# Queries and keys of the attention's second group as Strassen products behind the values, kept in DRAM

## The chip, the cores and the metric

The kernel runs on one core of a Trainium2 chip. A core has five engines: TensorE (PE: matrix products, with its weight loads listed apart as PEld), VectorE (DVE), ScalarE (ACT), GpSimd (POOL) and SyncE (SP), which here issues every DMA. Each engine works through its own instructions in program order, and engines wait for each other by semaphores. The metric is the device time of one execution in microseconds; the kernel before has a median of 1728.54 us over three runs (1725.78 to 1728.69).

## What is computed

A trunk of two layers over a sequence of 1024 rows of width 1024 in float32. The first layer is attention with three dilation groups (windows of 128, 512 and 2048 at dilations 1, 4 and 16), 16 heads of 64; the second is a state-space layer. The change touches the first.

```python
def dilated_attention_mixer(h, w_in, w_out, rel_bias):
    proj = h @ w_in                       # 1024 x (9 * 1024 + 1024)
    qkv = proj[..., :9 * 1024].reshape(B, S, 3, 3, 16, 64)   # q/k/v, group, head
    z = proj[..., 9 * 1024:]
    for g, (window, dilation) in enumerate(((128, 1), (512, 4), (2048, 16))):
        o, l = dilated_group_attention(qkv[:, :, 0, g], qkv[:, :, 1, g],
                                       qkv[:, :, 2, g], rel_bias, window, dilation)
        outs.append(o); lses.append(l)
    wts = softmax(stack(lses), axis=0)
    o = sum(wts[..., None] * stack(outs), axis=0)
    return (o * silu(z)) @ w_out
```

`dilated_group_attention` takes each residue of the position modulo the dilation by itself, in blocks of 128 queries against the same and the previous block of keys, with a bias, a mask, the softmax and its log-sum.

## The kernel before

**Precision.** A float32 factor is split into two parts, hi and lo, in a rounded 32-bit type (`split`: ACT casts the hi part, L83; DVE or POOL subtracts it for the lo part, L84). A product of two split factors takes three matmuls (hi·hi, hi·lo, lo·hi). `h` is held split in SBUF as `hh` and `hl`.

**The V phase** (`v_phase`, roughly the first 345 us) normalises and transposes the rows and computes the values of all groups and the gates. From the second chunk on the values are Strassen products (`Quads.values`): the operands are cut in quarters, `quad` makes seven products of quarters instead of eight, with sums of weight quarters on DVE ahead of each and sums of results behind it. It goes to DRAM (`v_dr`). Preparations for the second layer (`prep.powers`, `prep.products`) are hung on the running count of products, on products 8 + 3·et and 10 + 3·et.

**The attention** (roughly 345 to 1155 us) loops over eight pairs of heads, `attn_pair`. In a pair, for each of three groups g:

- The query weights are loaded (`load_w`, `wraw`, 512 KB on SP), split (`whi` on ACT, `wlo` on POOL), and multiplied: two halves of 24 matmuls 128x512 (`proj_half`, L110), each into a `psj` bank, of which there are two. `evac_q` (L200/201) scales, reorders by residue and splits the result into `qh`/`ql`. The same for the keys (`evac_k`: kh L83, kl L84, L214).
- `load_bias` loads a bias tile `T`, `load_v` the values `vp`, which are split to `vs`.
- Two units u = 0, 1 of four query tiles each (`attn_unit`): scores (L485, bank `psl`), bias and maximum on DVE (L488), exponentials on ACT (L499; each also shows as a read of its accumulator), transposes on PE (L510, `pt`), split into `ph` (hi on ACT, lo on DVE), the product with the values (L559 or L585, `pso`), copied to `O` by ACT (L569) and added there by DVE (L570).
- `put_ms` transposes maxima and sums (`ptm`, L597) and stores them (L604 in the last group).

**The merge** of a pair runs inside the next one: `merge_weights` loads maxima and sums (`cm`, L620), makes weights and stores them (L633); when the next pair comes to its second group, `merge` loads them three times (`mw`, L648, two DMAs each), multiplies the three `O` on POOL (L697) and adds them (L699). There are four `O` buffers, so the next pair's second `O` cannot be written before POOL has freed one.

**Order.** The scheduler fixes each engine's order when the program is built. It places weight splits and evacuations early, as they carry a high priority (`AHEAD`). All DMAs are issued on SP's one queue, in program order.

Of the kernel before, what the change touches and what calls it, by code (L numbers as in the profile page):

```python
# [15 lines left out]
F32 = mybir.dt.float32  # L16
# [7 lines left out]
P = 128  # L24
# [3 lines left out]
H = 512  # L28
NEG = -1.0e30
EPS = 1e-6  # L30

AHEAD = 600

# [146 lines left out]
def load_bias(c, p, g):  # L180


    t = c.attn.tile([P, 2, 256], F32, tag="T", name="T", bufs=2)
    at = 0 if g < 2 else P
    src = bass.AP(c.vec_dr.tensor, c.vec_dr.offset + (g * 16 + 2 * p) * 384 + at, [[1, P], [384, 2], [1, 256 - at]])
    c.nc.sync.dma_start(t[:, :, at:256], src)
    return t
# [26 lines left out]
            c.nc.scalar.copy(dh[HEADS[1 - s]], sv[HEADS[s]])  # L214


def zero_other(c, t):

    for s in range(2):
        rows = HEADS[1 - s]  # L220
        c.nc.gpsimd.tensor_copy(t[rows, s, :], c.zt[rows].to_broadcast([64, S]))


def load_first(c, a, k):
# [35 lines left out]
class Quads:  # L260
# [4 lines left out]
    def __init__(self, c):  # L265
        nc = c.nc
        self.c = c

        def part(th, kh):
            return [t[:, 4 * kh:4 * kh + 4, :] for t in c.h[th]]  # L270

        add, sub = ALU.add, ALU.subtract

        def tt(o, x, y, op):
            nc.vector.tensor_tensor(o, x, y, op=op)

# [24 lines left out]
        t2, t3 = c.vslot(2, F32), c.vslot(3, F32)  # L301
        self.sums = [t2[:, 0:2], t2[:, 2:4], t3[:, 0:2]]
        self.tmp = t3[:, 2:4].rearrange("p a x -> p (a x)")


    done, jobs = 0, {}

    def quad(self, raw, order, product, banks, use):
# [3 lines left out]
        c, nc = self.c, self.c.nc  # L312
        b11, b12, b21, b22 = raw
        n = b11.shape[2]
        tmp = self.tmp[:, 0:4 * n].rearrange("p (k x) -> p k x", k=4)

        def sub(o, x, y):
            nc.vector.tensor_tensor(o, x, y, op=ALU.subtract)
# [79 lines left out]
        self.quad(quarters, [0, 1, 5, 6, 4, 3, 2], product, banks, use)  # L398


def gates(c, a, h, es):
# [36 lines left out]

def load_v(c, p, g):
# [18 lines left out]
def ms_col(g, n, h, qt):  # L458

    return (n * 16 + h * 8 + 7 - qt, n * 16 + h * 8 + (qt ^ 1), n * 16 + h * 8 + qt)[g]  # L460


def attn_unit(c, g, u, q, k, v, bt, ms, O):
# [7 lines left out]
    for j in range(4):  # L471
        qt = u * 4 + j
        m = (7 - qt, 1 - qt % 2, 0)[g]
        start = (max(m - 1, 0) * P, qt // 2 * 256, qt * P)[g]
        w = 256 if m else 128
        tiles.append(w)
        ps = c.psl.tile([P, 2, 256], F32, tag="psl", name="psl")
# [6 lines left out]
        for n, (o, a, b) in enumerate(jobs):  # L484
            nc.tensor.matmul(o, a[:, qs], b, start=n == 0, stop=n == len(jobs) - 1, skip_group_check=True)  # L485
        for h in range(2):
            col = ms_col(g, 0, h, qt)
# [148 lines left out]
def big(c, p, name):  # L636

    if p == 7:
        return c.wraw.tile([P, S], F32, tag="wraw", name=name)
    return c.attn.tile([P, S], F32, tag="mw", name=name, bufs=2)  # L640


def weights_of(c, p, g):
# [5 lines left out]
    return w  # L649


def attn_pair(c, p, w_in, h):
    nc = c.nc
    c.pair = p
    O = []
    for g in range(3):
        qh = c.attn.tile([P, S], F32R, tag="qh", name="qh", bufs=2)
        ql = c.attn.tile([P, S], F32R, tag="ql", name="ql", bufs=2)
        w = load_w(c, w_in[g * 8 + p])
        for th in range(2):  # L660
            src = proj_half(c, w, h[th])
            with c.tc.high_priority(AHEAD):
                evac_q(c, src, g, th * H, (qh, ql))
        bt = load_bias(c, p, g)
        if g == 2:
            zero_other(c, c.kh)
        w = load_w(c, w_in[(3 + g) * 8 + p])
        for th in range(2):
            src = proj_half(c, w, h[th])
            with c.tc.high_priority(AHEAD):  # L670
                evac_k(c, src, g, th * H, c.kh, c.kl)
# [38 lines left out]
def attention(c, a):  # L710
# [36 lines left out]
    zt = c.cst.tile([P, 1], F32, name="zt")  # L747
    nc.vector.memset(zt, 0.0)
    c.zt = zt
    zero_other(c, c.kl)  # L750
    c.w_engine = nc.gpsimd
    for p in range(8):
        attn_pair(c, p, a["w_in"], h)
# [702 lines left out]
def trunk(tc, a):  # L1456
# [4 lines left out]
    with ExitStack() as es:  # L1461
# [12 lines left out]
        dram = lambda name, shape: c.dr.tile(shape, F32, name=name)  # L1474
        c.vec_dr = dram("vec_dr", [3, 16, 384])
        c.v_dr = dram("v_dr", [3, 2, S, H])
        c.ms_dr = dram("ms_dr", [8, 3, 4, S])
        c.wt_dr = dram("wt_dr", [8, 3, 2, S])
        c.on_dr = dram("on_dr", [8, P, S])
# [137 lines left out]
```

## Time and profile before

| what | value |
|---|---|
| median of three runs | 1728.54 us |
| the profiled execution's own time | 1722.86 us |
| its span in the trace | 1721.1 us |
| PE busy | 1655.9 us (96%) |
| DVE busy | 1064.8 us (62%) |
| ACT busy | 799.9 us (46%) |
| POOL busy | 483.5 us (28%) |
| moved by DMA | 212.68 MB |
| one head pair, from one store of L604 to the next | 96.6 us |

In a line of the timeline stand the start in us, the time, the engine, the line of the kernel, what is written from what, the shapes and how many were taken together, and in brackets the idle time ahead and who ended it. A matmul's own duration overlaps the next one's; what one costs is the distance from start to start.

### The profile page before, as it was taken

How to read it: one execution, taken by the hardware profiler on the slowest of the kernel's cores; microseconds unless marked ns; L12 is line 12 of the kernel's file. 1: busy time of each engine (PE TensorE's matmuls, PEld its weight loads, DVE VectorE, ACT ScalarE, POOL GpSimd, SP SyncE). 2: the span in 40 equal slices, each digit the busy share in tenths (PEclk: the TensorE clock that was granted, in tenths of full speed). 3: DMA queues.
4: the chain of work that ended last, by engine and by line, in shares of the span. 5: the costliest groups of instructions: out<-in, count | busy, mean ns of one | idle time of the engine just before them, and what ended most of it. 6: DMA issues, size and time to landing. Idle time of an engine off the chain costs nothing. (4 is left out here: it accounts for less than half of the span.)

```text
span 1721.1 us, 25792 instructions
## 1 busy us (share of the span) xinstructions
PE 1655.9 (96%) x9262; PEld 1415.1 (82%) x9262; DVE 1064.8 (62%) x2582; ACT 799.9 (46%) x1872; POOL 483.5 (28%) x321
## 2 busy tenths in 40 slices
PE   6999999999999999999999999988998999989998
PEld 5889999988888788888888888876886887867886
DVE  7698798735566556566555565557462777764533
ACT  5232222246656656656756756653442232243411
POOL 2000000041242432524342442405210344413121
PEclk9999999999999999999999999999999999999999
DMA  6223454441242323323232423327259766465432
GB/s 236 91 52 102 137 181 154 128 144 53 55 111 80 87 80 91 88 74 105 79 107 73 116 81 98 112 71 200 86 166 232 206 211 219 139 186 167 141 122 86
DMA packets 176900, 212.68 MB, mean 124 GB/s; under 512 B 37361, under 2 KB 133380, under 8 KB 176772
## 3 DMA queue, kind: packets, MB, share of 16 engines
q1 hardware_dynamic: 176772, 211.04, 40.9%
q8 instruction: 73, 1.20, 0.3%
q14 instruction: 55, 0.45, 0.1%
HBM read 154.03 MB, written 56.96 MB: 123 GB/s over the span
## 5 line engine op out<-in xcount | busy, mean ns | idle before, releaser
L110 PE MATMUL psj<-hh,whi 128*128 128x512 f32 x896 | 360.4, 402 | 16.2 <-ACT kh L214 8.5
L110 PE MATMUL psj<-hh,wlo 128*128 128x512 f32 x896 | 359.6, 402 | 0.3 <-POOL wlo L84 0.3
L110 PE MATMUL psj<-hl,whi 128*128 128x512 f32 x896 | 357.9, 399 | 0.0
L110 PEld LDWEIGHTS psj<-hh,whi 128*128 128x128 f32 x896 | 169.8, 189 | 51.6 <-ACT kh L214 10.6
L84 POOL TENSOR_TENSOR wlo<-wraw,whi 128x1024 fp32r<-128x1024 f32 x48 | 115.4, 2405 | 335.7 <-ACT whi L83 329.4
L110 PEld LDWEIGHTS psj<-hh,wlo 128*128 128x128 f32 x896 | 169.6, 189 | 35.8 <-POOL wlo L84 0.7
L110 PEld LDWEIGHTS psj<-hl,whi 128*128 128x128 f32 x896 | 169.8, 190 | 33.5
L499 ACT ACTIVATE lg<-lg,nm 128x128 f32<-128x128 f32 (+1 forms) x384 | 168.1, 440 | 18.9 <-DVE nm L494 18.0
L83 ACT CAST whi<-wraw 128x1024 fp32r<-128x1024 f32 x80 | 83.8, 1047 | 141.9 <-PE psj L110 97.4
L488 DVE CUSTOM_DVE_ANT_0 lg<-psl,T 128x128 f32<-128x128 f32 (+1 forms) x384 | 115.8, 346 | 53.5 <-PE psl L485 52.1
L84 DVE TENSOR_TENSOR ph<-pt,ph 128x512 fp32r<-128x512 f32 (+2 forms) x160 | 97.2, 621 | 37.4 <-ACT ph L83 35.3
L389 PE MATMUL psq<-whi,v 128*128 128x256 f32 x640 | 118.7, 283 | 0.0
L110 PE MATMUL psj<-h1h,whi 128*128 128x512 f32 (+1 forms) x272 | 107.0, 394 | 10.3 <-DVE z L1402 7.9
L84 DVE TENSOR_TENSOR kl<-psj,kh 64x512 fp32r<-64x512 f32 x96 | 66.0, 688 | 70.7 <-ACT kh L83 70.0
L570 DVE TENSOR_TENSOR O<-O,pso 64x512 f32<-64x512 f32 x64 | 44.2, 691 | 103.3 <-ACT O L569 102.6
L110 PE MATMUL psj<-h1l,whi 128*128 128x512 f32 (+1 forms) x272 | 105.4, 388 | 0.2 <-DVE h1l L84 0.2
L110 PE MATMUL psj<-h1h,wlo 128*128 128x512 f32 (+1 forms) x272 | 105.0, 387 | 0.0
L389 PEld LDWEIGHTS psq<-whi,v 128*128 128x128 f32 x640 | 99.5, 189 | 1.0 <-ACT whi L83 0.6
L83 ACT CAST ph<-pt 128x512 fp32r<-128x512 f32 (+2 forms) x160 | 81.6, 533 | 35.9 <-PE pt L510 34.7
L510 PE MATMUL pt<-identr,lg 128*128 128x128 f32 x560 | 93.5, 275 | 0.0
L559 PE MATMUL pso<-ph,vs 128*128 128x256 f32 (+1 forms) x544 | 89.9, 275 | 2.8 <-ACT ph L83 1.5
L559 PEld LDWEIGHTS pso<-ph,vs 128*128 128x128 f32 x544 | 81.6, 189 | 13.1 <-ACT ph L83 2.6
(287 smaller groups left out, 3862.7 us busy)
## 6 DMA issues: line engine op xcount, KB each, us to landing
wraw<-in_w_in_dram SPq DMA_DIRECT2D x56, 512.0 KB
mw<-wt_dr SPq DMA_DIRECT2D x48, 256.0 KB
v<-in_w_v_dram SPq DMA_DIRECT2D x20, 512.0 KB
vp<-v_dr SPq DMA_DIRECT2D x16, 512.0 KB
wraw<-in_ssm_w_in_dram SPq DMA_DIRECT2D x16, 512.0 KB
v_dr<-v SPq DMA_DIRECT2D x30, 256.0 KB
rot_dr<-rt SPq DMA_DIRECT2D x48, 128.0 KB
ca_dr<-ca SPq DMA_DIRECT2D x32, 144.0 KB
```

The lines of the kernel that those rows point to most:

```text
L83: nc.scalar.copy(hi, src)
L84: return (engine or nc.vector).tensor_tensor(lo, src, f32(hi), op=ALU.subtract)
L110: nc.tensor.matmul(ps, a[:, s], b[:, k, :], start=first and k == 0 and n == 0, stop=k == KT - 1 and n == 2, skip_group_check=True)
L389: nc.tensor.matmul(o, r[x][:, k, ts], w[y][:, k, :], skip_group_check=True, start=i in (0, 4, 5) and t % 2 == k == n == 0, stop=k == 3 and ...
L488: nc.vector.tensor_tensor_reduce(lg[:, h, j, 0:w], ps[:, h, 0:w], bt[:, h, 256 - w:256], scale=1.0, scalar=-3.0e38, op0=ALU.add, op1=ALU.m ...
L499: nc.scalar.activation(lg[:, h, j, 0:w], lg[:, h, j, 0:w], AF.Exp, bias=nm[:, h, b:b + 1], accum_out=ms[:, col:col + 1])
L510: c.nc.tensor.transpose(pt[:, n * P:(n + 1) * P], lg[:, h, j, part * P:part * P + P], c.ident)
L559: nc.tensor.matmul(o, l, r, start=n == 0, stop=n == len(jobs) - 1, skip_group_check=True)
L570: nc.vector.tensor_tensor(dst, dst, fr[1], op=ALU.add)
```

## The change

The queries and keys of the second group (g = 1, `MADE`) are no longer computed in `attn_pair`. They are computed right behind the values, in the V phase, by a new `Quads.tiles`: for each pair it loads its query and its key weights (two tiles of 512 KB), and makes seven Strassen products of quarters, each of 12 matmuls 128x512, where the attention had four halves of 24. Results are scaled, put in order by residue and split (`put_q`, `put_k`, `halves`), and stored hi and lo in DRAM (`q_dr`, `kk_dr`; ten DMAs and 2 MB a pair). The attention loads them per unit, eight DMAs and 1.25 MB each, into `mq`, `mkh` and `mkl`, of which there is one buffer each (`load_made`). Three other buffers change: `ph` has two instead of three, `mw` one instead of two, and `T` takes a slot of the ring with the tag "a", which has three. The preparations are hung on products 8 + 5·et and 11 + 5·et.

```diff
+MADE = 1
@@ load_bias
-    t = c.attn.tile([P, 2, 256], F32, tag="T", name="T", bufs=2)
+    t = c.slot("T", tag="a").rearrange("p (h x) -> p h x", h=2)
+def halves(c, p, src, scale=None):
+    if p < 6:
+        t = c.wraw.tile([P, 2, H], F32R, tag="wraw", name="qks")
+        hi, lo = t[:, 0], t[:, 1]
+    else:
+        hi, lo = (c.slot(x, F32R, tag="b") for x in ("qkh", "qkl"))
+    hi, lo = (x.rearrange("p (r l) -> p r l", r=src.shape[1]) for x in (hi, lo))
+    split(c, hi, lo, src, scale)
+    return hi, lo
+def put_q(c, p, th, t):
...
+    hi, lo = halves(c, p, t.rearrange("p (l r) -> p r l", r=o)[:, :, ::-1], 0.125)
...
+    for x in range(2):
+        nc.sync.dma_start(bass.AP(dr.tensor, off + x * 192 * S, [[S, 64]] + cols), f32(hi[HEADS[x]]))
+    nc.sync.dma_start(bass.AP(dr.tensor, off + 64 * S, [[S, P]] + cols), f32(lo))
+def put_k(c, p, th, t):
...
+    for x, v in enumerate(halves(c, p, t.rearrange("p (l r) -> p r l", r=o))):
+        off = c.kk_dr.offset + (p * 2 + x) * P * S + th * n
+        c.nc.sync.dma_start(bass.AP(c.kk_dr.tensor, off, [[S, P], [S // o, o], [1, n]]), f32(v))
+def load_made(c, p, u):
+    q, kh, kl = c.made
+    cols = slice(u * H, u * H + H)
+    for x in range(2):
+        nc.sync.dma_start(f32(q[:, x]), c.q_dr[p, x, :, cols])
+    for x in range(2):
+        for rows in HEADS:
+            nc.sync.dma_start(f32(kh[rows, x]), c.kk_dr[p, 0, HEADS[x], cols])
+        nc.sync.dma_start(f32(kl[HEADS[x], x]), c.kk_dr[p, 1, HEADS[x], cols])
+    return (q[:, 0], q[:, 1]), (kh, kl)
@@ class Quads
+    def tiles(self, srcs, use):
+        self.turn ^= 1
+        raw = c.vslot(10 + self.turn, F32).rearrange("p (n a) x -> p n (a x)", n=2)
+        for n, s in enumerate(srcs):
+            nc.sync.dma_start(raw[:, n], s)
...
+        def product(i, r, w, acc):
+            for k in range(4):
+                for n, (x, y) in enumerate(((0, 0), (0, 1), (1, 0))):
+                    nc.tensor.matmul(acc[0], w[x][:, k, :], r[y][:, k, :], skip_group_check=True,
+                                     start=i in (0, 4, 5) and k == n == 0, stop=k == 3 and n == 2)
...
+        self.quad(quarters, [0, 5, 1, 6, 4, 3, 2], product, banks, lambda th, nh, b, t: use(th, nh, t))
@@ v_phase
-        q.jobs.setdefault(8 + 3 * et, []).append(lambda et=et: prep.powers(et))
-        q.jobs.setdefault(10 + 3 * et, []).append(lambda et=et: prep.products(et))
+        q.jobs.setdefault(8 + 5 * et, []).append(lambda et=et: prep.powers(et))
+        q.jobs.setdefault(11 + 5 * et, []).append(lambda et=et: prep.products(et))
     for ch in range(2, 6):
         q.values(a, ch)
+    for p in range(8):
+        q.tiles([a["w_in"][(3 * x + MADE) * 8 + p] for x in range(2)],
+                lambda th, nh, t, p=p: (put_k if nh else put_q)(c, p, th, t))
@@ split_weights
-    t = c.attn.tile([P, 2, H], F32R, tag="ph", name="ph", bufs=3)
+    t = c.attn.tile([P, 2, H], F32R, tag="ph", name="ph", bufs=2)
@@ big
-    return c.attn.tile([P, S], F32, tag="mw", name=name, bufs=2)
+    return c.attn.tile([P, S], F32, tag="mw", name=name, bufs=1)
@@ attn_pair (the projections moved to queries_keys)
     for g in range(3):
+        if g != MADE:
+            q, k = queries_keys(c, p, g, w_in, h)
         bt = load_bias(c, p, g)
...
         for u in range(2):
-            attn_unit(c, g, u, (qh, ql), (c.kh, c.kl), v, bt, ms, O)
+            if g == MADE:
+                q, k = load_made(c, p, u)
+            attn_unit(c, g, u, q, k, v, bt, ms, O)
```

**What the engines run now.** Of the three places shown, the first is PE's queue in the fourth pair before the change, at the values' products of the second group. L559 is the product with the values (into `pso`), L510 the transposes, L485 the scores of the third group's first unit, L110 its projections:

```order
L110 MATMUL psj<-hh_111,wlo 128x512
L559 MATMUL pso<-ph,vs 128x256
L110 MATMUL psj<-hh_111,whi 128x512
L110 MATMUL psj<-hl_112,whi 128x512
L110 MATMUL psj<-hh_111,wlo 128x512
L110 MATMUL psj<-hh_111,whi 128x512
L559 MATMUL pso<-ph,vs 128x256 x3
L559 MATMUL pso<-ph,vs 128x128
L510 MATMUL pt<-identr,lg 128x128 x4
L559 MATMUL pso<-ph,vs 128x128 x3
L510 MATMUL pt<-identr,lg 128x128 x2
```

Eighteen projection matmuls stand ahead of these rows without a break, and fifteen more follow six score rows behind them. The same place of PE's queue after the change (L644 is the product with the values, L595 the transposes, L570 the scores of the third group, L112 the projections):

```order
L644 MATMUL pso<-ph,vs 128x256 x4
L644 MATMUL pso<-ph,vs 128x128
L595 MATMUL pt<-identr,lg 128x128 x4
L644 MATMUL pso<-ph,vs 128x128 x3
L595 MATMUL pt<-identr,lg 128x128 x2
L570 MATMUL psl<-kh,qh 128x2x128
L570 MATMUL psl<-kl,qh 128x2x128
L570 MATMUL psl<-kh,ql 128x2x128
L570 MATMUL psl<-kh,qh 128x2x128
L570 MATMUL psl<-kl,qh 128x2x128
L570 MATMUL psl<-kh,ql 128x2x128
L644 MATMUL pso<-ph,vs 128x256 x4
```

Seven projection matmuls and two score tiles stand ahead of these rows; within them, from one L644 with four matmuls to the next, there is no projection, and none comes before two more rows of transposes behind them. On ACT, the rows before the change at the same place (L83 casts the hi parts, L569 copies to `O`, L499 are the exponentials of the third group's first unit, L200 evacuates queries of the next pair):

```order
L83 CAST ph<-pt 128x512
L569 COPY O_7224<-pso 64x2x2x128
L83 CAST ph<-pt 128x256
L83 CAST whi<-wraw 128x1024
L200 ACTIVATE qh<-psj 64x512
L499 ACTIVATE lg,ms<-lg,nm 128x128 x6
L200 ACTIVATE ql<-psj 64x512
L499 ACTIVATE lg,ms<-lg,nm 128x128 x2
L610 COPY mt<-ptm 32x128
L569 COPY O_7224<-pso 64x2x2x128
```

The exponentials stand behind the last `ph` cast of the second group there. After the change (L85 casts, L654 copies to `O`, L584 are the same exponentials, L216 copies keys):

```order
L654 COPY O_7733<-pso 64x8x64
L85 CAST vs<-vp 128x16x64
L85 CAST ph<-pt 128x512
L85 CAST ph<-pt 128x256
L85 CAST kh<-psj 64x512
L584 ACTIVATE lg,ms<-lg,nm 128x128 x8
L85 CAST whi<-wraw 128x1024
L216 CAST kh<-psj 64x512
L85 CAST kh<-psj 64x512
L85 CAST ph<-pt 128x512
L654 COPY O_7975<-pso 64x2x2x128
L85 CAST ph<-pt 128x256
```

Eight exponentials, a weight cast and two evacuations of keys now stand between the second and the third `ph` cast. Of SP's queue, the piece behind a pair's end, before:

```order
L604 DMA ms_dr<-mt 32x128
L1280 DMA rot_dr<-rt 256x1x128
L620 DMA cm_1517<-ms_dr 64x6x32
L449 DMA vp<-v_dr 128x4x128 x2
L633 DMA wt_dr<-cm_1518 64x3x32
L648 DMA mw<-wt_dr 64x1024
L95 DMA wraw<-in_w_in_dram 128x1024
L648 DMA mw<-wt_dr 64x1024 x3
L186 DMA T<-vec_dr 128x2x128
L648 DMA mw<-wt_dr 64x1024 x2
```

And after (L705 is `cm`, L718 the store of the weights, L262, L265 and L266 the loads of `load_made`):

```order
L689 DMA ms_dr<-mt 32x128
L705 DMA cm_1519<-ms_dr 64x6x32
L265 DMA mkh<-kk_dr 64x512
L262 DMA mq<-q_dr 128x512 x2
L265 DMA mkh<-kk_dr 64x512
L266 DMA mkl<-kk_dr 64x512
L265 DMA mkh<-kk_dr 64x512 x2
L531 DMA vp<-v_dr 128x4x128 x2
L266 DMA mkl<-kk_dr 64x512
L97 DMA wraw<-in_w_in_dram 128x1024
L1375 DMA rot_dr<-rt 256x1x128 x2
L718 DMA wt_dr<-cm_1520 64x3x32
```

A unit's eight loads now stand between `cm` and the store of the merge's weights; the six loads of `mw` follow behind it, of which the third pair comes after the second unit's loads have begun.

More of the change, by code (lines that the diff above doesn't have):

```diff
@@ L303, in __init__ @@
         self.tmp = t3[:, 2:4].rearrange("p a x -> p (a x)")
+        self.turn = 0
     done, jobs = 0, {}
@@ L314, in quad @@
         n = b11.shape[2]
-        tmp = self.tmp[:, 0:4 * n].rearrange("p (k x) -> p k x", k=4)
+        tmp = self.tmp[:, self.turn * H:self.turn * H + 4 * n].rearrange("p (k x) -> p k x", k=4)
         def sub(o, x, y):
@@ L398, in values, with banks @@
         self.quad(quarters, [0, 1, 5, 6, 4, 3, 2], product, banks, use)
+    def tiles(self, srcs, use):
+        c, nc = self.c, self.c.nc
+        self.turn ^= 1
+        raw = c.vslot(10 + self.turn, F32).rearrange("p (n a) x -> p n (a x)", n=2)
+        for n, s in enumerate(srcs):
+            nc.sync.dma_start(raw[:, n], s)
+        raw = raw.rearrange("p n (k x) -> p n k x", k=KT)
+        quarters = [raw[:, nh, 4 * kh:4 * kh + 4] for kh in range(2) for nh in range(2)]
+        def banks(n):
+            pool, tag = ((c.psj, "psj"), (c.psl, "psl"), (c.pso, "pso"))[n]
+            return [pool.tile([P, H], F32, tag=tag, name="psq")]
+        def product(i, r, w, acc):
[3 more added lines that the diff above has]
+                                     start=i in (0, 4, 5) and k == n == 0, stop=k == 3 and n == 2)
+        turn = self.turn
+        self.at = lambda s, b: s[:, turn]
+        self.quad(quarters, [0, 5, 1, 6, 4, 3, 2], product, banks, lambda th, nh, b, t: use(th, nh, t))
 def gates(c, a, h, es):
@@ L474, in attn_unit @@
         start = (max(m - 1, 0) * P, qt // 2 * 256, qt * P)[g]
+        if g == MADE:
+            qt, start = j, start - u * H
         w = 256 if m else 128
@@ L486, in attn_unit @@
         for h in range(2):
-            col = ms_col(g, 0, h, qt)
+            col = ms_col(g, 0, h, u * 4 + j)
             nc.vector.tensor_tensor_reduce(
@@ L649, in weights_of, with queries_keys @@
     return w
+def queries_keys(c, p, g, w_in, h):
+    q = [c.attn.tile([P, S], F32R, tag=t, name=t, bufs=2) for t in ("qh", "ql")]
+    w = load_w(c, w_in[g * 8 + p])
+    for th in range(2):
+        src = proj_half(c, w, h[th])
+        with c.tc.high_priority(AHEAD):
+            evac_q(c, src, g, th * H, q)
+    if g == 2:
+        zero_other(c, c.kh)
+    w = load_w(c, w_in[(3 + g) * 8 + p])
+    for th in range(2):
+        src = proj_half(c, w, h[th])
+        with c.tc.high_priority(AHEAD):
+            evac_k(c, src, g, th * H, c.kh, c.kl)
+    return q, (c.kh, c.kl)
 def attn_pair(c, p, w_in, h):
@@ L656, in attn_pair @@
     for g in range(3):
[L657 to L663, printed above, removed]
-        bt = load_bias(c, p, g)
[L665 to L671, printed above, removed]
+        if g != MADE:
+            q, k = queries_keys(c, p, g, w_in, h)
+        bt = load_bias(c, p, g)
         v = load_v(c, p, g)
@@ L749, in attention @@
     c.zt = zt
-    zero_other(c, c.kl)
+    c.made = [c.attn.tile([P, 2, H], F32R, tag=f"m{x}", name=f"m{x}") for x in ("q", "kh", "kl")]
+    for t in (c.kl, c.made[2]):
+        zero_other(c, t)
     c.w_engine = nc.gpsimd
@@ L1476, in trunk @@
         c.v_dr = dram("v_dr", [3, 2, S, H])
+        c.q_dr = dram("q_dr", [8, 2, P, S])
+        c.kk_dr = dram("kk_dr", [8, 2, P, S])
         c.ms_dr = dram("ms_dr", [8, 3, 4, S])
```

12 lines of the change are left out of this document (11 added, 1 removed).

## The prediction

> **What bounds the kernel now.** I read the page first (busy times), then the windows of the two stages that the change touches.
>
> ```profile
> span 1721.1 us, 25792 instructions
> PE 1655.9 (96%) x9262; PEld 1415.1 (82%) x9262; DVE 1064.8 (62%) x2582; ACT 799.9 (46%) x1872; POOL 483.5 (28%) x321
> ...
> 250.00:300.00 50.00, 50.00 (x417) 48.34 (x416) 41.92 (x65) 13.88 (x23) 2.28 (x4) 1.00 0.54 165
> 500.00:1100.00 600.00, 591.51 (x3334) 507.50 (x3333) 345.47 (x1021) 387.04 (x1038) 237.51 (x128) 1.00 0.32 91
> ```
>
> A row of windows gives the stretch, its length, the busy time of PE, PEld, DVE, ACT and POOL, the granted clock, and the DMA's share and rate. In the Strassen part of the V phase (250 to 300) PE never rests; in the attention (500 to 1100) it rests 8.5 of 600 us. Both stages are bound by PE, so a matmul taken out is worth its pitch, as long as no other engine becomes late. ACT and DVE have room on average (387 and 345 of 600 us), but each works through its queue in order, so what counts is what stands ahead of the work PE waits for. The waits of PE in 500 to 1100 are few:
>
> ```profile
> PE psj L110 <- ACT kh L214: 7.7, 3, 2.6
> PE pso L559 <- DVE ph L84: 0.7, 2, 0.3
> ```
>
> Nearly all of its rest is for key evacuations on ACT. The span and 1.8 us around it make the profiled execution's 1722.86 us; the median of the runs is 1728.54, 5.7 us above. I make the sum against 1722.86 and add 5.7 at the end.
>
> **Pitches.** A row of the timeline: start, time, engine, line, names; a run of one kind is one row.
>
> ```profile
> 602.15 1.15 PE L559 MATMUL pso<-ph,vs 128*128 128x256 f32 x9
> 603.13 0.95 PE L510 MATMUL pt<-identr,lg 128*128 128x128 f32 x7
> 603.84 0.37 PE L485 MATMUL psl<-kh,qh 128*128 128x256 f32 x1
> 605.07 0.39 PE L110 MATMUL psj<-hh,whi 128*128 128x512 f32 x1
> 608.10 0.39 PE L110 MATMUL psj<-hl,whi 128*128 128x512 f32 x1
> ...
> 611.41 0.28 PE L485 MATMUL psl<-kh,ql 128*128 128x256 f32 x1
> 611.53 0.28 PE L485 MATMUL psl<-kl,ql 128*128 128x256 f32 x1
> ```
>
> From start to start: nine value products in 0.98 us (0.109 each), seven transposes in 0.71 (0.10), thirteen projections between 605.07 and 608.10 (3.03 / 13 = 0.233), a score 0.12.
>
> **1. PE's saving.** Out go 8 pairs x 4 halves x 24 = 768 projections, in come 8 x 7 x 12 = 672 of the same size: 96 x 0.233 = **−22.4 us**. The V phase grows by 672 x 0.233 = 156.6 us, the attention shrinks by 179.
>
> **2. The new V-phase tiles stay on PE.** A tile's 84 matmuls take 19.6 us. DVE does beside them four differences and seven lo parts of weights, five sums of results and four lo parts of output, 20 operations of 128x512.
>
> ```profile
> L361 DVE TENSOR_TENSOR v<-v,psq 128x512 f32<-128x512 f32 x6 | 4.1, 687 | 2.0 <-PE psq L389 2.0
> ```
>
> 20 x 0.69 = 13.8 us, under 19.6. The preparations spread to every fifth product lie in part beside these tiles and take some of the 5.8 us left. ACT has less than DVE. Ten stores and two loads a tile (3 MB in 19.6 us, 153 GB/s) lie under the 165 GB/s that the window 250 to 300 carried. I take +1, bounds −2 (better than now there is little to win, PE is full) and +8 (1 us a tile, if evacuation and banks do not mesh).
>
> **3. ACT is bunched at the second group's value products.** This carries the forecast. In the attention the 96 projections of the second group were also filler between PE's waits. In the order after the change, PE has in the fourth pair, from the last value product of the first group to the second `L644` x4 row, three transposes, two scores, seven projections, six scores, four plus one plus three value products, six transposes and six scores: 0.3 + 0.24 + 1.63 + 0.72 + 0.44 + 0.1 + 0.3 + 0.6 + 0.72 = 5.1 us. ACT must do in that time, in the order shown, everything from the copy to `O` to the third `ph` cast:
>
> ```profile
> L499 ACT ACTIVATE lg<-lg,nm 128x128 f32<-128x128 f32 x179 | 69.7, 391 | 5.7 <-DVE nm L494 5.6
> L499 ACT ACTIVATION_READ_ACCUMULATOR lg<-lg,nm 128x1 f32 x329 | 62.0, 189 | 0.0
> L83 ACT CAST ph<-pt 128x512 fp32r<-128x512 f32 x98 | 55.7, 586 | 21.0 <-PE pt L510 20.4
> L83 ACT CAST kh<-psj 64x512 fp32r<-64x512 f32 x84 | 48.9, 582 | 27.9 <-PE psl L485 14.5 <-DVE kl L84 10.8 <-PE psj L110 1.5
> L83 ACT CAST whi<-wraw 128x1024 fp32r<-128x1024 f32 x42 | 43.9, 1046 | 16.8 <-issue 11.8 <-PE psj L110 3.1 <-DMA vp<-v_dr 1.8
> L214 ACT CAST kh<-psj 64x512 fp32r<-64x512 f32 x56 | 32.5, 580 | 29.6 <-DVE kl L84 29.1
> L569 ACT COPY O<-pso 64x512 f32<-64x512 f32 x56 | 32.4, 579 | 52.5 <-PE pso L559 51.5
> L83 ACT CAST vs<-vp 128x1024 fp32r<-128x1024 f32 x21 | 22.0, 1050 | 0.3
> ...
> L83 ACT CAST ph<-pt 128x256 fp32r<-128x256 f32 x28 | 10.4, 370 | 8.3 <-PE pt L510 8.2
> ```
>
> A group's row ends with busy time, mean of one in ns, and idle ahead. O 0.58, vs 1.05, ph 0.59 and 0.37, kh 0.58, eight exponentials with their accumulator reads 8 x (0.391 + 0.189) = 4.64, whi 1.05, two kh 1.16, ph 0.59: 10.6 us. PE has 5.1, so it waits 5.5. Behind that, ACT does O, ph, kh, five exponentials and kh (0.58 + 0.37 + 0.58 + 2.9 + 0.58 = 5.0 us) before the next projection bank is free, against some 1.5 us on PE: 3.5 more. Together 9.0. The same bunch stands in seven of the eight pairs (not in the second); ACT's excess alone, without PE's handoffs, is 5.1 to 7.9 us in them, some 47 us together, with the second step up to 63. I take 8 each: **+56 us**, bounds +30 (the pairs' ACT is ahead of PE when the bunch begins) and +63. Before, the exponentials stood behind the last cast, and projections stood between; the 8.5 us of rest there go with the old order: **−8.5**.
>
> The waits are paid in full, since ACT's lateness falls on PE, and nothing else on PE is late then that they could overlap.
>
> **4. The loads of the second unit.** `mq`, `mkh` and `mkl` have one buffer, so the second unit's loads start when the first unit's last score has read it. On SP, two loads take 1.24 us to issue, and a load's way to its reader shows in the third `mw` load:
>
> ```profile
> 575.19 1.24 SPq L449 DMA_DIRECT2D vp<-v_dr  x2
> 580.97 0.61 SPq L633 DMA_DIRECT2D wt_dr<-cm  x1
> 582.94 8.96 SPq L648 DMA_DIRECT2D mw<-wt_dr  x6
> 590.81 1.09 SPq L648 DMA_DIRECT2D mw<-wt_dr  x2
> ...
> 588.38 4.75 POOL L697 TENSOR_TENSOR O<-O,mw 128x1024 f32<-128x1024 f32 x2 [7.55 <-DMA mw<-wt_dr]
> 595.86 2.40 POOL L697 TENSOR_TENSOR O<-O,mw 128x1024 f32<-128x1024 f32 x1 [2.72 <-DMA mw<-wt_dr]
> 598.34 4.88 POOL L699 TENSOR_TENSOR O<-O,O 128x1024 f32<-128x1024 f32 x2
> ```
>
> 590.81 to 595.86 is 5.05 us, of which 1.09 issues. The first score of the second unit needs five loads: 5 x 0.6 + 4 = 7 us at the most, 5.5 with the shorter issue of 0.34. PE has 6.6 to 8.2 us of projections and others between (counted in the order at the pitches; 28 projections are 6.5). So 0 to 1 us a pair; bounds 0 and 3, that is 0 and +24. I take +2 for eight. `T` from a ring slot and two `ph` buffers cost nothing by the same view: both are written well ahead of their readers, and DVE and ACT take `ph` one at a time.
>
> **Sum.** 1722.86 − 22.4 + 1 + 56 − 8.5 + 2 = 1751.0 us for a profiled execution; + 5.7 = **1757** on the scale of the median.
>
> **The clock as a rival.** After long rests PE runs at half speed here:
>
> ```profile
> 596.56 0.50 PE L110 MATMUL psj<-hh,whi 128*128 128x512 f32 x1 [2.57 <-ACT kh L214]
> 1164.09 0.80 PE L110 MATMUL psj<-hh,whi 128*128 128x512 f32 x1 [7.65 <-DVE tz L801]
> 1164.68 0.63 PE L110 MATMUL psj<-hl,whi 128*128 128x512 f32 x1
> 1168.10 0.49 PE L110 MATMUL psj<-hh,whi 128*128 128x512 f32 x1
> ...
> 594.00:596.00 2.00, 0.00 (x0) 0.00 (x0) 0.06 (x1) 1.95 (x8) 0.14 (x1) 1.00 0.46 90
> 1162.00:1164.00 2.00, 0.00 (x0) 0.00 (x0) 1.97 (x6) 0.88 (x2) 0.00 (x0) 0.50 1.01 274
> 1166.00:1168.00 2.00, 2.00 (x6) 1.63 (x5) 1.54 (x5) 1.58 (x4) 0.00 (x0) 0.50 1.18 314
> 1168.00:1170.00 2.00, 2.00 (x9) 1.59 (x9) 2.00 (x3) 0.66 (x2) 1.57 (x1) 0.93 1.13 303
> ```
>
> A rest of 2.57 us left the clock at 1.00; one of 7.65 us brought it to 0.50 until 1168, and eight projections from 1164.68 to 1168.10 took 0.43 each instead of 0.233, 1.6 us lost. The wait of 5.5 us lies between these two. If each of the seven places loses 1.6 us: +11, so **1768**.
>
> [...]
>
> **The merge as a rival.** With one `mw` buffer the three weight loads follow each other. Before, from the transpose of the maxima to the end of POOL's first addition it took from 570.76 to 600.8 (half of 4.88 after 598.34), 30 us:
>
> ```profile
> 570.76 0.27 PE L597 MATMUL ptm<-identr,ms 128*32 128x128 f32 x1
> ```
>
> With one buffer the second and third load each wait for the multiplication before, some 3.7 us more each: 37 us, and more where SP's queue has the unit's eight loads ahead (8 x 0.6 = 4.8). ACT's second copy to `O` needs the buffer which that addition frees, and ACT is in order. In the shortened pair that copy comes 37 to 47 us behind the transpose. So the price is 0 as long as the chain stays under 37 us, and some 4 us a pair at 41: 7 x 4 = 28, **1785**. I take 0 in the forecast, as the cover also grows by the waits of part 3.
>
> **The other side.** If ACT is ahead of PE at the bunches (its exponentials done before PE gets there), the waits stay as small as now and the saving remains: 1728.54 − 22.4 + 1 + 2 + 3 for small waits = **1712**, faster. The point is whether ACT has used 5.5 us of rest ahead of the bunch. For it speaks that ACT rests 213 of 600 us; against it that the copy to `O` at the head of the list cannot run before PE's product. And waits of 2 to 3 us a place would just eat up the saving: 7 x 2.8 = 20, no change.
>
> **Chances.** The forecast 1757: 0.49. Clock 1768: 0.17. Merge 1785: 0.13. Bunch absorbed, 1712: 0.14. Cancelled, about 1728: 0.07. The range 1722 to 1785 holds the first three and the cancelled case and leaves out the absorbed one and the worse half of the merge's, some 2 in 10. A difference of 0.2% is about what a measurement of this kernel can tell from none. Faster by more 0.15, within 0.06, slower 0.79.
>
> **What would show it.** Step 1: 672 matmuls of the new line in the V phase, which ends about 157 us later, and a head pair's PE work at 74 us. Step 3: waits of PE's value products for the `ph` cast or its lo part, and of projection banks for the kh copy, together 40 to 60 us, in seven places that lie between the second group's transposes; a head pair of 80 to 82 us instead of 96.6. Step 4: the first score of the second unit waits for `mkh`/`mq` under 1 us. Clock: a granted clock under 1.00 behind these places. Merge: ACT's `O` copy waiting for POOL. Wrong it would be if PE rests under 20 us in the attention (absorbed), or rests mostly for DMA.

## The result

The changed kernel takes 1790.43 us (median of four runs, 1783.7 to 1793.31), the kernel before 1727.16 in the same number of runs. The ratio is 1.0362 with a 95% interval of 1.0329 to 1.0396: slower by 63 us. The forecast had the sign and 1757, the range ended at 1785. The profiled execution took 1793.31 us, its span is 70.4 us longer than that of before.

The page of the changed kernel, span and busy times:

```profile
span 1791.5 us, 26244 instructions
## 1 busy us (share of the span) xinstructions
PE 1674.9 (93%) x9166; PEld 1429.1 (80%) x9166; DVE 1165.2 (65%) x2678; ACT 805.2 (45%) x1864; POOL 451.7 (25%) x307
```

PE has 96 matmuls less and is still busy for 19 us more. That points to a slower clock, and the windows say where. I cut both executions where the first `vs` cast starts (357 and 514) and where the last pair ends (1156 and 1223). The kernel before:

```profile
0.00:357.00 357.00, 341.42 (x2379) 310.77 (x2380) 281.77 (x606) 108.44 (x161) 26.19 (x28) 1.00 0.45 140
357.00:1156.00 799.00, 787.60 (x4394) 673.54 (x4393) 453.62 (x1331) 509.64 (x1369) 287.52 (x159) 1.00 0.30 86
1156.00:1721.00 565.00, 526.86 (x2492) 430.80 (x2490) 329.46 (x645) 181.84 (x345) 169.77 (x134) 0.98 0.55 166
```

And the changed kernel:

```profile
0.00:514.00 514.00, 496.06 (x3046) 433.47 (x3046) 398.03 (x765) 185.63 (x264) 28.98 (x30) 1.00 0.48 146
514.00:1223.00 709.00, 647.59 (x3628) 561.33 (x3628) 442.16 (x1269) 437.70 (x1258) 255.09 (x143) 0.94 0.41 114
1223.00:1791.00 568.00, 531.23 (x2493) 434.31 (x2493) 324.97 (x645) 181.89 (x343) 167.63 (x134) 0.97 0.55 166
```

The V phase grew by 157 us and stays at full clock; the rest behind the attention by 3. The attention shrank by only 90 us, though 766 matmuls less run in it (4394 − 3628; 766 x 0.233 = 178 us). PE rests there for 709 − 647.6 = 61.4 us instead of 11.4, which is 50 us, and the mean granted clock is 0.94 instead of 1.00. 178 − 50 − 90 leaves 38 us for the slower clock. The trace's clock record agrees: it has thirteen stretches at half clock there, 88.7 us together, and PE is busy for 72.0 us of them, half of which, 36 us, is my estimate of what they cost at a granted clock of 0.50.

What PE waits for in the attention of the changed kernel (us in total, times, longest):

```profile
PE pso L644 <- DVE ph L86: 17.8, 14, 2.6
PE pso L644 <- DVE vs L86: 12.3, 5, 4.7
PE psj L112 <- DVE kl L86: 8.2, 2, 7.0
PE psl L570 <- DMA mkl<-kk_dr: 6.2, 3, 2.2
PE psl L570 <- DVE ms L573: 5.0, 7, 1.2
PE pso L644 <- ACT ph L85: 4.2, 2, 2.1
```

Many waits of about 2 us, more than half of their sum at the value products. In the third pair the place looks like this on PE (only the rows with rest ahead of them), with the windows of 4 us beside it:

```profile
763.42 0.35 PE L644 MATMUL pso<-ph,vs 128*128 128x256 f32 x1 [3.62 <-DVE vs L86]
764.05 1.12 PE L644 MATMUL pso<-ph,vs 128*128 128x256 f32 x4 [0.28 <-DVE ph L86]
767.72 0.55 PE L570 MATMUL psl<-kh,qh 128*128 128x256 f32 x1 [0.70 <-DVE ms L573]
771.63 1.12 PE L644 MATMUL pso<-ph,vs 128*128 128x256 f32 x4 [2.08 <-DVE ph L86]
...
760.00:764.00 4.00, 0.35 (x1) 0.19 (x1) 3.97 (x3) 3.92 (x19) 3.92 (x2) 0.98 0.55 110
764.00:768.00 4.00, 3.25 (x14) 2.88 (x15) 1.85 (x10) 2.53 (x5) 3.92 (x3) 0.50 0.00 0
768.00:772.00 4.00, 1.92 (x8) 1.63 (x8) 3.01 (x12) 1.93 (x7) 3.70 (x2) 0.50 0.79 241
772.00:776.00 4.00, 4.00 (x15) 3.42 (x15) 1.75 (x4) 3.92 (x16) 0.00 (x0) 0.50 0.80 240
```

The waits shown add to 6.7 us; the clock is at half from 764 to 776, through work and further waits alike.

The longest of these four waits, and the longest of the whole attention (for `kl`, 7.0 us), stand behind single DVE operations that took far longer than usual:

```profile
759.90 3.37 DVE L86 TENSOR_TENSOR vs<-vp,vs 128x1024 fp32r<-128x1024 f32 x1
...
713.13 7.18 DVE L579 TENSOR_SCALAR nm<-ms 128x8 f32<-128x8 f32 x1
722.13 0.80 PE L112 MATMUL psj<-hh,whi 128*128 128x512 f32 x1 [7.00 <-DVE kl L86]
```

The `vs` split usually takes 1.22 us; here POOL multiplies for the merge from 759.81 to 762.18 beside it. L579 negates the maxima of a unit and usually takes 0.19 us; here POOL goes through casts, a weight split and rotations without a pause until 720.27, and L579 ends at 720.31. Two `kl` operations stand behind it on DVE, and PE waits for the second.

### The profile page after: what moved, and what is told of

The parts are those of the page before. It is cut to its first block, busy times and chain, and to the rows that moved or that the text cites. A ratio compares the mean times of both kernels' runs of the same rounds, so it can differ in the third digit from the quotient of the medians.

```text
span 1791.5 us, 26244 instructions
## 1 busy us (share of the span) xinstructions
PE 1674.9 (93%) x9166; PEld 1429.1 (80%) x9166; DVE 1165.2 (65%) x2678; ACT 805.2 (45%) x1864; POOL 451.7 (25%) x307
## 5 line engine op out<-in xcount | busy, mean ns | idle before, releaser
L112 PE MATMUL psj<-hh,whi 128*128 128x512 f32 x640 | 263.9, 412 | 18.0 <-DVE kl L86 8.2
L112 PE MATMUL psj<-hl,whi 128*128 128x512 f32 x640 | 260.1, 406 | 0.0
L112 PE MATMUL psj<-hh,wlo 128*128 128x512 f32 x640 | 259.5, 406 | 0.0
L584 ACT ACTIVATE lg<-lg,nm 128x128 f32<-128x128 f32 (+1 forms) x384 | 168.3, 441 | 63.4 <-DVE nm L579 63.0
L112 PEld LDWEIGHTS psj<-hh,whi 128*128 128x128 f32 x640 | 125.5, 196 | 44.2 <-DVE kl L86 8.6
L85 ACT CAST whi<-v 128x512 fp32r<-128x512 f32 (+1 forms) x91 | 71.6, 787 | 184.9 <-PE psq L443 110.1
L86 POOL TENSOR_TENSOR wlo<-wraw,whi 128x1024 fp32r<-128x1024 f32 x32 | 76.9, 2405 | 300.3 <-ACT whi L85 260.9
L112 PEld LDWEIGHTS psj<-hh,wlo 128*128 128x128 f32 x640 | 124.4, 194 | 26.9
L112 PEld LDWEIGHTS psj<-hl,whi 128*128 128x128 f32 x640 | 125.4, 196 | 24.7
L85 ACT CAST whi<-wraw 128x1024 fp32r<-128x1024 f32 x64 | 67.1, 1048 | 160.4 <-PE psj L112 107.7
L644 PE MATMUL pso<-ph,vs 128*128 128x256 f32 (+1 forms) x544 | 103.4, 302 | 35.3 <-DVE ph L86 17.8
L644 PEld LDWEIGHTS pso<-ph,vs 128*128 128x128 f32 x544 | 87.1, 207 | 46.1 <-DVE ph L86 21.7
L112 PE MATMUL psj<-h1h,whi 128*128 128x512 f32 (+1 forms) x272 | 107.9, 397 | 9.7 <-DVE z L1497 7.9
L112 PE MATMUL psj<-h1l,whi 128*128 128x512 f32 (+1 forms) x272 | 106.3, 391 | 0.2 <-DVE h1l L86 0.2
L112 PE MATMUL psj<-h1h,wlo 128*128 128x512 f32 (+1 forms) x272 | 105.8, 390 | 0.0
L86 DVE TENSOR_TENSOR wlo<-v,whi 128x512 fp32r<-128x512 f32 (+1 forms) x91 | 81.4, 894 | 26.7 <-ACT whi L85 26.2
L595 PE MATMUL pt<-identr,lg 128*128 128x128 f32 x560 | 95.1, 293 | 0.3 <-ACT mt L695 0.3
L85 ACT CAST ph<-pt 128x512 fp32r<-128x512 f32 (+2 forms) x160 | 82.0, 529 | 24.7 <-PE pt L595 22.7
```

What stands on the lines that cost most here:

```text
L85: nc.scalar.copy(hi, src)
L86: return (engine or nc.vector).tensor_tensor(lo, src, f32(hi), op=ALU.subtract)
L112: nc.tensor.matmul(ps, a[:, s], b[:, k, :], start=first and k == 0 and n == 0, stop=k == KT - 1 and n == 2, skip_group_check=True)
L584: nc.scalar.activation(lg[:, h, j, 0:w], lg[:, h, j, 0:w], AF.Exp, bias=nm[:, h, b:b + 1], accum_out=ms[:, col:col + 1])
L595: c.nc.tensor.transpose(pt[:, n * P:(n + 1) * P], lg[:, h, j, part * P:part * P + P], c.ident)
L644: nc.tensor.matmul(o, l, r, start=n == 0, stop=n == len(jobs) - 1, skip_group_check=True)
```

## The experiments

Four theories stood against each other: the lost projections had been a cushion that covered PE's many short waits, and the waits bring the clock down with them (1); the smaller buffers make things late (2); the loads do (3); the waits are there whatever PE has to do (4). Later came the merge (5) and one unlucky order (6).

**The buffers alone.** The kernel before with

```diff
-    t = c.attn.tile([P, 2, 256], F32, tag="T", name="T", bufs=2)
+    t = c.slot("T", tag="a").rearrange("p (h x) -> p h x", h=2)
-    t = c.attn.tile([P, 2, H], F32R, tag="ph", name="ph", bufs=3)
+    t = c.attn.tile([P, 2, H], F32R, tag="ph", name="ph", bufs=2)
-    return c.attn.tile([P, S], F32, tag="mw", name=name, bufs=2)
+    return c.attn.tile([P, S], F32, tag="mw", name=name, bufs=1)
```

> The kernel before with the three buffer edits alone (one mw buffer, two ph buffers, T in a ring slot), queries and keys of the second group still projected in the attention. Theory 1 (the projections that stood between the second group's value products are gone, so ACT's and DVE's queue there becomes PE's rest, and rests of some 2 us bring the clock to half): within 6 us of the kernel before (1727), PE rests under 20 us in the attention. Theory 2 (the smaller buffers make the merge and the splits late, wherever the projections are): 1750 or more, with PE waiting for DVE's vs and ph and several stretches at half clock.

1726.75 us, ratio 0.9986 (0.9975 to 0.9997): in the old order the smaller buffers cost nothing. Its attention:

```profile
357.00:1157.00 800.00, 788.87 (x4396) 674.78 (x4394) 454.00 (x1332) 508.24 (x1368) 288.06 (x159) 1.00 0.30 86
```

11.1 us of rest, as before. Theory 2 is out as a cause of its own.

**Half the pairs.**

```diff
...
-        if g != MADE:
+        made = g == MADE and p < 4
+        if not made:
             q, k = queries_keys(c, p, g, w_in, h)
...
-    for p in range(8):
+    for p in range(4):
```

> The change for the first four pairs alone; pairs five to eight project their second group in the attention as before, with the changed buffers. Theory 1: half the loss, 1727 + 31 = about 1759; the pairs with loads take some 87 us and hold all the half-clock stretches, the last four take 96 to 98 us at full clock. Theory 2 (buffers): the last four pairs show rests and half clock too, over 101 us each, and the whole is 1775 or more.

1764.29 us, 1.0202 (1.0179 to 1.0224): a little more than half the loss. Three pairs that load and the last two, which project, in windows:

```profile
562.00:821.00 259.00, 237.32 (x1340) 205.08 (x1339) 163.97 (x472) 166.39 (x479) 93.03 (x51) 0.94 0.40 110
1002.00:1198.00 196.00, 192.02 (x1070) 164.51 (x1069) 112.76 (x330) 119.83 (x331) 65.62 (x35) 0.99 0.32 91
```

A loading pair rests 7.2 us ((259 − 237.3) / 3) at a clock of 0.94, a projecting one 2 us at 0.99 (2.1 over all four of them, 821 to 1198), with the same buffers in the same execution. What makes the difference goes with the projections.

**The exponentials behind.** My working had put the blame on eight exponentials between two `ph` casts on ACT, so they went behind. `c.ph_cast` is the last `ph` cast that the program has made up to there, so the edit also holds the third group's second unit behind the casts of its first:

```diff
+        c.hi_cast = nc.scalar.copy(hi, src).ins
...
+    c.ph_cast = c.hi_cast
...
+            with c.tc.issue_after(c.ph_cast) if g == 2 else nullcontext():
+                nc.scalar.activation(lg[:, h, j, 0:w], lg[:, h, j, 0:w], AF.Exp, bias=nm[:, h, b:b + 1],
+                                     accum_out=ms[:, col:col + 1])
```

> The change, with the exponentials of the third group put behind the last ph cast of the second group on ACT; nothing else is touched, the other engines' orders follow by the scheduler. Theory 1: PE's rest in the attention falls from 61 to under 30 us, half-clock stretches from twelve to four or fewer, time 1715 to 1745. Theory 2 (buffers) or theory 3 (the loads from DRAM hold everything up): 1775 or more, as many half-clock stretches as now.

1784.71 us, 1.032 (1.0302 to 1.0338), only 6 us less. This part of theory 1 missed. The waits moved:

```profile
PE psl L570 <- DVE ms L573: 21.4, 11, 6.7
PE pso L646 <- DVE vs L86: 8.5, 4, 4.9
PE pso L646 <- DVE ph L86: 5.7, 9, 2.3
...
711.86 7.10 DVE L579 TENSOR_SCALAR nm<-ms 128x8 f32<-128x8 f32 x1
```

Waits for DVE's part of `ph` fell from 17.8 to 5.7 us, so most of these had hung on the exponentials. But those of the scores for DVE's reduction (`ms`) rose from 5.0 to 21.4, and PE rests 55.5 us in the attention instead of 61.4. The longest of the new waits are not for ACT: 6.73 us stand behind the L579 of 7 us again, now with scores behind it, and three more of 2.7 to 2.9 us behind small DVE operations, L579 or those on `cm`, which took 2.1 to 3.4 us beside POOL. With nothing to put between, other waits show.

**One load instead of two.**

```diff
...
-            if g == MADE:
+            if g == MADE and u == 0:
                 q, k = load_made(c, p, u)
```

> The change, but the second unit of the second group uses the queries and keys of the first unit again: its eight loads are left out, all else is computed. Theory 1: only PE's waits for mkl and mkh (7 us) and the three half-clock stretches behind them go, 1775 to 1783. Theory 3 (the loads on SP's queue delay the merge's and the weights' loads and so most of the rests): 1755 or less.

1785.97 us, 1.032 (1.0296 to 1.0345): 4 us less. PE's rest in the attention falls by 7 us, the waits for these loads, to 54.2; but thirteen stretches at half clock remain, not ten, so theory 1 had expected a little too much too. Theory 3 is out.

**Useless work.** The most direct test of the cushion:

```diff
-def proj_half(c, w, h):
+def proj_half(c, w, h, times=1):
...
-    proj_part(c, ps, w, h, range(KT))
+    for _ in range(times):
+        proj_part(c, ps, w, h, range(KT))
...
-        src = proj_half(c, w, h[th])
+        src = proj_half(c, w, h[th], 1 + (g == 2))
```

> The change, with useless work for PE: each half of the third group's queries and keys is multiplied twice into the same bank, 96 more projections a pair, 768 in all (179 us at 0.233), as many as the change took out of the attention; no other engine gets work. Theory 1 (the projections were a cushion that filled PE's waits, and the waits and the half clock are there because it is gone): rests of PE in the attention fall from 61 to under 25 us and half-clock stretches there from thirteen to five or fewer, so the time rises by only 179 - 36 - 25 = about 118 us, to 1900 to 1920. Theory 4 (the waits come from the loads, the merge and the order on ACT and DVE, whatever PE has to do): all of it on top, 1960 to 1970.

1871.29 us, 1.0829 (1.0813 to 1.0845): 81 us more than the changed kernel for 179 us of added PE work, less even than theory 1 had it. Its attention, and all that PE waits for there:

```profile
514.00:1303.00 789.00, 785.11 (x4400) 675.48 (x4400) 400.69 (x1269) 437.41 (x1258) 249.22 (x143) 1.00 0.38 103
...
PE psj L112 <- DVE ql L204: 3.1, 1, 3.1
PE psl L571 <- DMA mkh<-kk_dr: 1.6, 3, 0.7
PE psl L571 <- DMA mkl<-kk_dr: 0.2, 1, 0.2
...
L86 DVE TENSOR_TENSOR vs<-vp,vs x24: 1220/1224/1226, 513.7 to 1285.6; 128x1024 fp32r<-128x1024 f32 x24
```

Rest 3.9 us, clock 1.00. The same loads, the same merge, the same work on ACT: the waits are not theirs alone, they show when PE has too little to do between them. Theory 4 (1960 to 1970) is out. What the run does not tell apart is how the work helps. It can lie over waits that are still there, and it also lengthens the pair, so that the other engines meet less: DVE does the same 1269 operations in 400.7 us instead of 442.2, and no `vs` split (minimum, median and maximum in ns in the last row) ran into POOL. No run separates the two. This run also gives a second figure for the clock's price: 785.1 − 772 x 0.233 = 605 us is the changed kernel's own PE work at full clock, where its own attention shows 647.6 busy: 42 us, near the 36 and 38 found above.

**Real work as a cushion.** The four gate projections of the V phase (48 matmuls each), moved:

```diff
...
-    gates(c, a, c.h, range(EARLY, 8))
...
         if g == 1:
             run_merge(c)
+            if p < 4:
+                gates(c, c.a, h, [EARLY + p])
```

> The change, with the four gate projections (48 matmuls each, with their loads and evacuations) moved from the start of the V phase into the first four pairs of the attention, at the second group. Nothing is computed twice. Theory 1: the first four pairs get half of their cushion back; their rests and half clock (some 45 us in all) fall by half to two thirds, time 1755 to 1775. Theory 4: no gain, or some us more for the new work on ACT and POOL, 1785 to 1800.

1775.14 us, 1.0269 (1.0239 to 1.03), at the edge of what was expected. In the attention it does what theory 1 says, but the V phase had needed these gates too:

```profile
0.00:498.00 498.00, 457.74 (x2854) 402.41 (x2854) 385.58 (x753) 177.42 (x252) 31.25 (x30) 0.98 0.47 142
498.00:1209.00 711.00, 676.76 (x3820) 583.20 (x3820) 435.87 (x1277) 443.05 (x1270) 265.71 (x147) 0.97 0.44 121
```

192 more matmuls (45 us) in the attention cost 2 us of length there; but the V phase, with 45 us less to do, is only 16 us shorter and rests 40 us instead of 18, at a clock of 0.98.

The same move on top of the run with half the pairs:

> The change for the first four pairs alone (as in the run with half the pairs) and the four gate projections moved into these pairs. Theory 1: half of the Strassen saving (11 us) stays, the loss of 35 us of the run with half the pairs shrinks to 10 to 20: 1738 to 1750. If the cushion has to be whole, or the waits have another cause: 1760 or more.

1765.12 us, 1.0216 (1.0191 to 1.024), nothing gained over half the pairs alone, and by the time on the rival's side. The windows say why: the attention does as theory 1 has it (its rest halves, from 34.1 us with half the pairs to 17.1), but the V phase rests 47.9 us instead of 25.0, at a clock of 0.96 instead of 0.99. The first `vs` split started at 418.0 instead of 434.0 us, 16 us earlier for 45 us of work moved, and the last pair ended where it had ended (1198.8, 1198.4).

**Forced rests.** This run shows after which rests the clock fell. After 24 products of the V phase of the kernel before, PE waits for a chain of copies on ACT:

```diff
+def rest(c, last, l, r, n):
...
+    with c.tc.issue_after(last):
+        nc.tensor.matmul(a[:, 0:P], l, r, start=True, stop=True, skip_group_check=True)
+    nc.scalar.copy(s[:, 0], a[:, 0:P])
+    for k in range(n):
+        nc.scalar.copy(s[:, (k + 1) % 2], f32(s[:, k % 2]))
+    return nc.tensor.matmul(b[:, 0:P], l, s[:, n % 2], start=True, stop=True, skip_group_check=True).ins
```

> The kernel before, with 24 forced rests of PE in the V phase, where it is otherwise always busy: after a product a small matmul, a chain of 3, 6, 9 or 12 copies of 128x128 on ACT in turn, and a small matmul that reads the last copy, ahead of the next product. Theory A (the clock falls when PE is busy for less than about half of one fixed window of 3.4 us, as the records of the changed kernel read): rests under 1.5 us leave the clock at 1.00, rests of 1.7 to 3 us bring it down at some places and not at others, rests over 3.4 us always, and each fall lasts a multiple of 3.4 us. Theory B (only a rest of over 3.4 us, a whole window, counts): nothing under 3.4 us brings it down.

1868.97 us in one run. Two rests of equal length, and the windows that follow each:

```profile
216.73 0.33 PE L270 MATMUL rest<-rest,v 128*128 128x128 f32 x1 [1.96 <-ACT rest L269]
264.94 0.33 PE L270 MATMUL rest<-rest,hh 128*128 128x128 f32 x1 [1.96 <-ACT rest L269]
...
218.00:220.00 2.00, 2.00 (x19) 2.00 (x18) 0.00 (x0) 0.00 (x0) 0.00 (x0) 1.00 0.81 262
266.00:268.00 2.00, 2.00 (x12) 1.47 (x10) 0.62 (x1) 0.19 (x1) 0.00 (x0) 0.58 0.00 0
268.00:270.00 2.00, 2.00 (x11) 2.00 (x11) 1.97 (x4) 1.71 (x4) 1.15 (x2) 0.57 0.06 14
```

The same 1.96 us left the clock alone at 216.73 and 315.75 and halved it at 264.94, 363.69 and 411.64; each of the 18 rests of 2.95 us or more came with half clock. The last of the 24 was cut by other matmuls into 1.13 and 0.33 us and left the clock alone, the only case under 1.5 us. Theory B is out.

**The merge left out** for the first seven pairs (no multiplications, by the gates neither, no additions and no loads of the merge's weights and gates; the third group is stored as it is):

```diff
-    for g in range(3):
-        engine = nc.vector if p == 7 else nc.gpsimd
-        engine.tensor_tensor(O[g], O[g], weights_of(c, p, g), op=ALU.mult)
-    for g in range(2):
+    for g in range(3 if p == 7 else 0):
+        nc.vector.tensor_tensor(O[g], O[g], weights_of(c, p, g), op=ALU.mult)
+    for g in range(2 if p == 7 else 0):
...
-    if p >= EARLY:
+    if p == 7:
```

> The change, with the merge left out for the first seven pairs: POOL's three multiplications and two additions and the loads of the merge's weights and gates; the third group's result is stored as it is. Theory 1 (missing cushion): only the part goes in which POOL's merge and DVE's all-SBUF work slow each other (the vs split took up to 3.37 us instead of 1.22), at most 11 us of rest and a few half-clock stretches, 1765 to 1782. Theory 5 (the merge with its one mw buffer sets the pair's length): 1745 or less.

1764.91 us, 1.0217 (1.0193 to 1.0241): 25 us less than the changed kernel, all that the collisions had been given. The `vs` splits on DVE in the changed kernel and, behind the dots, here (min/median/max in ns):

```profile
L86 DVE TENSOR_TENSOR vs<-vp,vs x24: 1209/1225/3372, 514.7 to 1215.6; 128x1024 fp32r<-128x1024 f32 x24
```

```profile
L86 DVE TENSOR_TENSOR vs<-vp,vs x24: 1209/1223/1227, 513.7 to 1188.7; 128x1024 fp32r<-128x1024 f32 x24
...
514.00:1196.00 682.00, 638.76 (x3628) 551.58 (x3628) 424.34 (x1269) 435.15 (x1257) 159.08 (x105) 0.96 0.36 100
```

So the merge is a part, 25 of 63 us with its share of the clock, and not the cause of the rest: 43 us of rest and a clock of 0.96 remain. The 7 us behind L579 are among them, since POOL's casts, weight splits and rotations are still there. No run takes those off POOL, so what DVE's delays beside POOL cost in all stays open.

**Other orders.** AHEAD, which says how early splits and evacuations are placed, at 60 and at 3000 instead of 600:

> The change with AHEAD = 60 instead of 600: weight splits and evacuations are placed less early, which gives another order on every engine and no other work. Theory 1: any order lacks the cushion, 50 to 70 us of PE rest in the attention, 1775 to 1810. Theory 6 (only this one order is unlucky): this one or the next at 1750 or less.

> The change with AHEAD = 3000 instead of 600: weight splits and evacuations are placed as early as they can be, again another order and no other work. Theory 1: 50 to 70 us of PE rest in the attention, 1775 to 1810. Theory 6: this one or the one before at 1750 or less.

1766.46 us (1.0229, 1.0197 to 1.0261) and 1778.94 us (1.0299, 1.0276 to 1.0322). The order is worth up to 24 us, more than I gave it, but no order came near 1750. At 60 PE rests 47.5 us in the attention, a little under the 50 to 70 expected, and no L579 takes over 2.3 us; at 3000 it rests 57.7:

```profile
514.00:1215.00 701.00, 643.33 (x3627) 556.74 (x3627) 441.21 (x1268) 436.31 (x1258) 254.91 (x143) 0.95 0.42 115
```

**Both mends** (exponentials behind, two gates moved):

> An attempt at a better version: the change, with the third group's exponentials behind the second group's last ph cast, and two of the four gate projections moved from the V phase into the first two pairs. Theory 1: the two gates bring back some 10 us of rest and half clock in these pairs and cost 5 in the V phase, so 1775 to 1782; not under the kernel before.

1771.11 us, 1.0247 (1.0231 to 1.0262). Better than expected by 4 us and still 43 above the kernel before. No version that was tried keeps the saving of the new products and beats the kernel before.

## Why the prediction was right in its sign and wrong in its size

- **PE's saving and the V phase** (−22.4, +1): right. The attention's first split starts 157 us later, as the 156.6 of the tiles and 1 gave.
- **The rests in the attention** (+56 and +2 less 8.5, so +49.5): the size came out, 61.4 − 11.4 = 50.0 us, but in part by luck. The 56 were to be waits for `ph` and for the banks behind `kh`, from ACT's bunch. For `ph` the value products at L644 waited 22.0 us (17.8 and 4.2); the largest others were 12.3 for `vs`, 7.0 behind L579, 7.0 for the loads and 5.0 for `ms`, and none of these was in the 56.
- **Where they come from** (part 3): half right. The second group's value products are where most of them lie, in the third pair 6.7 us where I took 8, but 3.62 of them are for `vs`. The eight exponentials were one cause among several: put behind, they took most of the waits for `ph` with them, and others left 55.5 of the 61.4 us. What is shown is the cushion: with useless projections back in the attention the rests are 3.9 us, and no other engine had less to do. Part of the rest (with its clock 25 us) comes from the merge, which now meets the second group's `vs` split (3.37 us beside it, 1.22 without). I had looked at the merge only as a chain that ends too late, with ACT's copies to `O` waiting for POOL, and no such wait is in the trace; it cost in another way, by holding up DVE.
- **The loads** (+2, bounds 0 and +24): small, 7 us of waits, 4 in time without the second unit's.
- **The clock** (0 in the sum, +11 in the rival): this step failed. I took from one rest of 2.57 us without a fall and one of 7.65 with it that a place's rest must be long in one piece, that seven places could fall at most, and that one fall costs 1.6 us. There were thirteen stretches at half clock in the attention, and they cost 36 to 42 us, some 3 each. With the forced rests one wait of 1.96 us was enough at three places of five. And here the stretch at half clock from 764 us, with waits of 0.70 and 2.08 us in it, lasted 13.7. The kernel before had it in its own attention, in the first pair, at just such a place:

```profile
397.94 0.39 PE L559 MATMUL pso<-ph,vs 128*128 128x256 f32 x1 [1.45 <-ACT ph L83]
398.91 0.63 PE L559 MATMUL pso<-ph,vs 128*128 128x256 f32 x3 [0.58 <-DVE ph L84]
...
400.00:402.00 2.00, 2.00 (x7) 1.53 (x7) 0.88 (x2) 1.90 (x4) 0.99 (x1) 0.57 0.00 0
```

Behind two waits of 1.45 and 0.58 us the clock was at half from 400.3 to 403.7; my working began at 500 us and missed them.

With the clock at its measured 38 the sum would have been 1751 + 38 + 3 behind the attention = 1792 for the profiled execution, which took 1793.3; that it comes so near rests on the luck with the rests.

## What to carry to other kernels

Work that fills a bound engine's short waits has a value beyond its own time: before moving it elsewhere, ask what will stand between the engine's waits, and test it by putting useless work there. Where PE's rests come in pieces of about 2 us, price them with stretches at half clock on top, not with the rest alone: here eighteen rests of 1.5 us or more came with thirteen stretches that cost some 3 us each. Look for single operations that take many times their usual time, too, as here L579 with 7.18 us instead of 0.19: what held it up shows in no queue's order. A place where work is taken from can need it as a cushion too, as the V phase needed its gates.

## What the runs showed of the hardware

**The clock fell after a rest of 1.96 us at three places of five.** In the clock records of the kernel before and of the changed one every stretch at half clock lasts 3.41 us or two, three or four times that, apart from the last of each, which runs past the end of the program. Laid on a grid of 3.41 us from the clock's own changes, PE's busy share, worked out from the starts and ends of its matmuls, was 0.00 to 0.54 in the 27 cells ahead of a fall, and 0.47 or more in the 946 cells at full clock that no fall followed; back to full speed it came only after cells of 0.89 or more, and it stayed at half after cells of 0.22 to 0.89. In these two traces it thus fell after every cell at full clock below 0.47 and after none above 0.54. With the forced rests, too, what 1.96 us did went with where they lay in the cells: of the two rows shown, the one at 264.94 lies in a cell of 0.43, the one at 216.73 in part in a cell of 0.53. And the 2.57 us that did nothing in the kernel before (to 596.56) spread over two, of 0.75 and 0.50.

**DVE's operations took longer beside POOL.** The `vs` split on DVE (128x1024, two operands in SBUF) took 1.22 us alone and up to 3.37 beside POOL's merge in the changed kernel, where six of 24 took over 1.23; without the merge none did. A small operation lost far more: in the attention of the kernel before and of the changed one the negation of the maxima (128x8, L494 and L579) took at most 0.17 us in the 30 and 22 cases where POOL was idle beside it, and beside POOL up to 2.36 and 7.18. The one of 7.18 us ended at 720.31, as POOL paused at 720.27 behind six operations.
